# An S5 and pooling block on one core: one gate product moved into the readout, modulation rows and context norm issued earlier

## Chip, cores and metric

The kernel runs on one core of a Trainium2 chip (the other cores are idle). The metric is the device time of one execution in microseconds. In the views, PE is TensorE (PEld its weight loads), DVE is VectorE, ACT is ScalarE, POOL is GpSimd, SP is SyncE, which here only issues DMAs; the granted clock of TensorE is given as a share of 2.4 GHz.

## What is computed

One layer over 1024 latent tokens and 256 context tokens, 1024 channels wide, all in float32 (cut):

```python
h  = modulate(rms_norm(x, norm1_g), sh1, sc1)        # sh1, sc1, g1, ...: sections of silu(c) @ w_mod + b_mod
hc = modulate(rms_norm(ctx, norm1_g), csh1, csc1)
proj, proj_c = h @ w_in, hc @ w_in[:, :512]          # w_in 1024 x 3072
u_a, u_b, gate_a, gate_b = split(proj, [512, 1024, 2048])
st_f, st_b = s5_states(u_a, ...)                     # complex diagonal scan, seeded from the context
y = gelu((c_f . st_f + c_b . st_b).real + d * u_a)   # "readout"
y_a = (y * sigmoid(y @ w_glu + b_glu)) @ w_branch_a  # "GLU", then branch a
y_b = pool_mixer(u_b) @ w_branch_b                   # windowed means, 4 products with pool_w, branch b
x = x + g1 * ((sigmoid(gate_a) * y_a + sigmoid(gate_b) * y_b) @ w_out)
x = x + g2 * swiglu(modulate(rms_norm(x, norm2_g), sh2, sc2), w_ffn_in, w_ffn_out)
out = rms_norm(x, final_norm_g)
```

## The kernel before

Channels lie on partitions, tokens on the free axis, in two halves of 512. Every float32 product is made of three products of rounded parts: each operand is split into a high part (an ACT copy with rounding) and a low part (a DVE subtraction), and `mm3` issues high by high, high by low and low by high (L264, L266, L268; 128x512 each).

**Weights.** `Weights` goes through a list of jobs (one DMA each) and of units (one rounding each: ACT L97, DVE L98), laid down in `weight_order`. `take(ahead)` hands out the next rounded unit and rounds further ones until `ahead` units are ready behind it. When the last unit of a job is rounded, `load` issues the DMA of the next job (L79, on SP). There are two raw buffers, and five `wt` buffers for rounded weights.

**Order.** The program is scheduled by hand: each engine does its instructions in the order in which the code is written. Work that runs beside a product is written as Python generators ("side"): a product calls `next(side)` after each of its k steps. DMAs are issued on the SP and ACT queues, each in order. Each hardware DMA takes the next of eight completion semaphores, which the two queues share, so an issue also waits until the DMA eight issues before it has landed.

**Stages** (times of the span). *Startup* (0 to 85 us): `x` is loaded, normed and transposed; rows of the modulation (`mod_rows(kp)`, matmuls L543 from `wm` tiles, three buffers, loaded by `load_mod`, L494) and columns (`mod_cols`, L553, then DVE L558) give the modulated `h` (ACT L470 and L471, DVE L472), and products `mm(kt, q)` (L579) with slabs of `w_in` (L501, three buffers) follow tile by tile. *Input projection* (to about 210): pooling, context norm (`scale_ctx` puts its DVE operations in a queue that `drain(n)` empties by n) and the matrices of the scan (`mats`). *Scan* to 350, with gate products `gate("b", ...)` and `gate("a", 0, 4)`, each eight k steps of `mm3`, two sigmoids (ACT L1316) and two stores (L1317, ACT queue). *Readout*, 351 to 383: `f_phase(m)` for m of 0 to 3, 48 small matmuls each (L1339 from `U` and `M`, L1341 from `Fw` and the states `V`), gelu (ACT L1343) into one tile `y`, and eight stores of `y` (L1348, SP queue). `Fw`, `M` and `U` have two buffers each, so `f_loads(m + 2)` is issued when phase m has read its own. *Late gates*, 387 to 445: gates a4 to a7, each followed by one pooling product `pool_mm`; beside them `tiles` loads and splits sixteen halves of the pooled differences `d` and of `y` (loads L1360, ACT L1366, DVE L1367), and `sections` does steps of modulation sections 2 to 4 (load of 256 KB from `w_mod`, three ahead, into one of eight `ld` buffers, then DVE L1428 or L1430). *Branches*, 445 to 550: four GLU products (L1513 to L1516: sigmoid; DVE add of the two parts of y; DVE multiplication; split), then eight rounds of branch b and branch a products and the merge, with section steps beside them; `gather_sections` in round 3 needs 32 steps done. *Output projection and SwiGLU* to the end.

Of the kernel before, what the change touches and what calls it, by code (L numbers as in the profile page):

```python
# [235 lines left out]
class Kernel:  # L236
# [81 lines left out]
    def run(self):  # L318
# [36 lines left out]
        with self.pool("fpool", side="right") as fp:  # L355
            loads = [self.f_loads(fp, m) for m in range(2)]
            self.gate("a", 0, 4, side)
            for _ in side:
                pass
            for m in range(4):  # L360
                self.f_phase(fp, m, loads)
        par.close()
        vs.close()
        self.ap1 = es.enter_context(self.pool("acts1", side="right"))
# [10 lines left out]
    def weight_order(self):  # L375
        W = self.W8 = Weights(self)
        cols = lambda w, c, n: w[:, c:c + n].rearrange("(k p) m -> p k m", p=128)
        two = [(0, 0), (0, 128)]
        w_in = self.w_in[0]
        W.units += W.job([cols(w_in, 896, 128)], 8, 128, [(0, 0)])  # L380
        for c in list(range(0, 512, 256)) + list(range(2048, 3072, 256)) + list(range(1024, 2048, 256)):
            W.units += W.job([cols(w_in, c, 256)], 8, 256, two)
            if c == 1280:
                W.units += W.job([self.pool_w[0].rearrange("j c m -> c j m")], 4, 128, [(0, 0)])
        W.units += W.job([cols(self.w_glu[0], 0, 512)], 4, 512, [(0, i * 128) for i in range(4)])
        for c in range(0, D, 256):
            W.units += W.job([cols(w[0], c, 256) for w in (self.w_branch_b, self.w_branch_a)], 4, 256,
                             [(s, i) for i in (0, 128) for s in (0, 1)])
# [85 lines left out]
    def startup(self, hs):  # L474
# [166 lines left out]
        scale(7, nc.scalar)  # L641
        load_slab(3)
        mm(0, 0)
        mm(1, 0)
        for u in self.ub:
            u.append(self.psum())
# [4 lines left out]
        slab(2)  # L651
        self.drain(10)
        mm(0, 1)
        mod_rows(1)
        load_mod(2, 0)
        load_mod(2, 1)
        self.s5_load_b()
        self.s5_load_c()
        trans(2, 0)
# [93 lines left out]
    def input_proj(self):  # L753
# [26 lines left out]
        pooling = pool_steps()  # L780
        for kt, q in ((6, 1), (7, 0), (7, 1)):
            self.mm_ub(kt, q)
            next(mats)
            self.drain(5)
        begin(0, self.ub[0])
        begin(1, self.ub[1])

# [542 lines left out]
    def f_phase(self, fp, m, loads):  # L1330
        nc = self.nc
        Fw, M, U = loads[m]
        y = fp.tile([128, 8, 128], F32, name="y")
        for hf in range(2):
            p = self.psum()
            for i in range(4):
                g = hf * 4 + i
                o = p[:, i * 128:i * 128 + 128]
                nc.tensor.matmul(o, M[:, i, hf], U[:, g], start=True, stop=False, skip_group_check=True)  # L1339
                for d in range(2):  # L1340
                    nc.tensor.matmul(o, Fw[:, d, g], self.V[d][:, d:d + 8, m * 8 + g, 0:16],  # L1341
                                     start=False, stop=(d == 1), skip_group_check=True)
            nc.scalar.activation(y[:, hf * 4:hf * 4 + 4].rearrange("p j (b i) -> p j i b", b=16),  # L1343
                                 p.rearrange("p (j i b) -> p j i b", j=4, b=16), AF.Gelu_apprx_tanh)
        if m < 2:
            loads.append(self.f_loads(fp, m + 2))
        for t in range(8):
            nc.sync.dma_start(self.yT[m][:, t].rearrange("(g c) n -> c g n", c=16), y[t * 16:t * 16 + 16])  # L1348


    def at1(self, dt=F32R):
# [92 lines left out]
    def late_gates(self):  # L1444
# [5 lines left out]
        def tiles():  # L1450

            srcs = []
            for kind, j in todo:
                for q in range(2):
                    srcs.append((kind, j, q, self.dT[j][:, q * 512:q * 512 + 512] if kind == "d" else
                                 self.yT[j][:, q * 4:q * 4 + 4].rearrange("p t n -> p (t n)")))
            got = [self.ld(srcs[i][3]) for i in range(3)]
            for i, (kind, j, q, _) in enumerate(srcs):
                if i + 3 < len(srcs):
# [15 lines left out]
        tiles = tiles()  # L1475
        sections = self.mod_sections((2, 3, 4))

        def side(n, m):
            for i in range(8):
                if i % 2 == 0 and i // 2 < n:  # L1480
                    next(tiles, None)
                elif m > 3 or i > 5:
                    next(sections, None)
                yield

        ph, pl = self.W8.take()
        for _ in range(2):
            next(tiles)
        for m in range(4, 8):
            self.gate("a", m, m + 1, side(4, m))  # L1490
            pool_mm(m - 4)
        self.sections = sections
        self.ys = [ys[m] for m in range(4)]

    def branch(self, acts, left, side=None):
        wh, wl = self.W8.take(min(2, left))
        ps = [self.psum() for _ in range(2)]
        for k in range(4):
            self.mm3(ps, wh[:, k], wl[:, k], acts[k], k == 0, k == 3)
            if side and k % 2:  # L1500
                next(side, None)
        return ps

    def branches(self):
        nc = self.nc

        ya = []
        for m in range(4):
            ps = self.branch(self.ys, 2, self.sections)
            ts = []  # L1510
            for q in range(2):
                t, u = self.ld(), self.ld()
                nc.scalar.activation(t, ps[q], AF.Sigmoid, bias=self.cols[:, 84 + m:85 + m])  # L1513
                hi, lo = self.ys[m][q]
                nc.vector.tensor_tensor(u, hi.bitcast(F32), lo.bitcast(F32), op=OP.add)
                nc.vector.tensor_tensor(t, t, u, op=OP.mult)  # L1516
                ts.append(t)
            ya.append([self.split_a(t, self.at2) for t in ts])
        merged = []
# [583 lines left out]
```

## Time and profile before

| | |
|---|---|
| runs before | median 1316.56 us of 3 (1312.87 to 1317.75) |
| profiled execution | 1315.17 us; span 1313.4 us |
| granted clock of TensorE, mean | 0.988 |
| busy PE, PEld, DVE, ACT, POOL | 1246.1, 1005.1, 948.5, 531.4, 13.4 us |
| HBM read, written | 168.67 MB, 70.00 MB |

The span reaches from the first to the last instruction; the execution's own time has 1.8 us more. Busy time counts an engine's own instructions. "Idle before, releaser" is the idle time of an engine just ahead of an instruction, and what ended it. A window row gives busy time per engine in a stretch, the mean granted clock there and the share of the DMA engines.

### The profile page before, as it was taken

What the parts mean: (1) busy time and instruction counts of PE and PEld (TensorE: products, weight loads), DVE (VectorE), ACT (ScalarE), POOL (GpSimd) and SP (SyncE); (2) the same over time, 40 slices, a digit from 0 to 9 for tenths busy, and PEclk for the clock granted to TensorE, in tenths of its full rate; (3) what the DMA queues carried; (4) which work ended last, traced back from release to release, by engine and by line L of the source; (5) the groups of instructions that cost most, each with busy time, mean ns of one, the idle gap of its engine ahead of it and who ended that gap; (6) DMA issues with size and microseconds to landing.
All of it is one profiled execution on the core that took longest, in us unless ns stands there. A gap on an engine that the chain in (4) does not pass through costs nothing.

```text
span 1313.4 us, 16704 instructions
## 1 busy us (share of the span) xinstructions
PE 1246.1 (95%) x5811; PEld 1005.1 (77%) x5811; DVE 948.5 (72%) x1778; ACT 531.4 (40%) x951; POOL 13.4 (1%) x36
## 2 busy tenths in 40 slices
PE   6888989999969999999999999999999999999996
PEld 4567757878868788788887788888888888888884
DVE  7779983899606696855679977678778766578576
ACT  5564214742225521222574333333333345454443
POOL 4000000000000000000000000000000000000000
PEclk8999999999989999999999999999999999999998
DMA  8624569126477665653514733676666539776543
GB/s 286 182 97 162 180 184 339 65 81 216 145 183 251 208 211 189 209 175 111 199 35 141 235 107 108 147 233 206 227 209 203 175 126 321 272 227 194 189 144 129
DMA packets 196428, 239.79 MB, mean 183 GB/s; under 512 B 16928, under 2 KB 117880, under 8 KB 195832
## 3 DMA queue, kind: packets, MB, share of 16 engines
q1 hardware_dynamic: 188200, 222.92, 52.8%
q10 hardware_dynamic: 8144, 15.80, 3.2%
q8 instruction: 46, 0.75, 0.2%
q14 instruction: 38, 0.31, 0.1%
HBM read 168.67 MB, written 70.00 MB: 182 GB/s over the span
## 4 chain that ended last, share of the span: by engine, by line
PE 59%; DVE 19%; DMA 9%; ACT 7%; issue 4%; SPq 1%; ACTq 0%; DVEq 0%
PE ps L1724 10%; PE ps L1722 10%; PE ps L1723 9%; PE ps L1953 5%; PE ps L1954 5%; PE ps L1952 5%; PE ps L268 2%; PE ps L264 2%; PE ps L266 2%; PE ps L1568 2%; PE ps L1566 2%; PE ps L1567 2%; DMA wm<-in_w_mod_dram 1%; DVE wt L98 1%; DMA Md<-kb 1%
## 5 line engine op out<-in xcount | busy, mean ns | idle before, releaser
L1722 PE MATMUL ps<-a,wt 128*128 128x512 f32 x436 | 172.7, 396 | 2.4 <-ACT ld L1836 2.4
L1724 PE MATMUL ps<-a,wt 128*128 128x512 f32 x436 | 171.5, 393 | 0.3 <-DVE wt L124 0.3
L1723 PE MATMUL ps<-a,wt 128*128 128x512 f32 x436 | 170.6, 391 | 0.0
L124 DVE TENSOR_TENSOR a<-a,a 128x512 fp32r<-128x512 f32 x162 | 103.3, 685 | 30.9 <-ACT a L225 30.2
L1953 PE MATMUL ps<-a,a 128*128 128x512 f32 x308 | 122.0, 396 | 1.1 <-DVE a L124 1.1
L1952 PE MATMUL ps<-a,a 128*128 128x512 f32 x308 | 121.8, 396 | 0.0
L1954 PE MATMUL ps<-a,a 128*128 128x512 f32 x308 | 121.8, 396 | 0.0
L264 PE MATMUL ps<-h,wt 128*128 128x512 f32 x336 | 109.0, 405 | 5.1 <-ACT wt L97 4.7
L268 PE MATMUL ps<-h,wt 128*128 128x512 f32 x336 | 105.4, 395 | 2.0 <-DVE wt L98 1.9
L266 PE MATMUL ps<-h,wt 128*128 128x512 f32 x336 | 105.0, 394 | 0.0
L225 ACT ACTIVATE a<-a 128x512 fp32r<-128x512 f32 x154 | 87.1, 624 | 42.9 <-DVE a L124 13.2
L1722 PEld LDWEIGHTS ps<-a,wt 128*128 128x128 f32 x436 | 81.8, 188 | 21.1 <-ACT ld L1836 3.3
L1724 PEld LDWEIGHTS ps<-a,wt 128*128 128x128 f32 x436 | 81.9, 188 | 20.4 <-DVE wt L124 1.2
L1723 PEld LDWEIGHTS ps<-a,wt 128*128 128x128 f32 x436 | 82.0, 188 | 18.4
L1366 ACT ACTIVATE a<-ld 128x512 fp32r<-128x512 f32 x64 | 39.3, 629 | 128.4 <-DVE ld L1543 64.9
L264 PEld LDWEIGHTS ps<-h,wt 128*128 128x128 f32 x336 | 60.3, 190 | 19.9 <-ACT wt L97 5.7
L268 PEld LDWEIGHTS ps<-h,wt 128*128 128x128 f32 x336 | 60.8, 189 | 16.6 <-DVE wt L98 4.6
L266 PEld LDWEIGHTS ps<-h,wt 128*128 128x128 f32 x336 | 61.7, 190 | 12.5
L98 DVE TENSOR_TENSOR wt<-raw,wt 128x1024 fp32r<-128x1024 f32 (+1 forms) x42 | 39.8, 951 | 43.5 <-ACT wt L97 43.4
L1953 PEld LDWEIGHTS ps<-a,a 128*128 128x128 f32 x308 | 57.9, 188 | 15.8 <-DVE a L124 1.9
L1952 PEld LDWEIGHTS ps<-a,a 128*128 128x128 f32 x308 | 57.9, 188 | 14.0
L1954 PEld LDWEIGHTS ps<-a,a 128*128 128x128 f32 x308 | 57.9, 188 | 13.9
(336 smaller groups left out, 2456.0 us busy)
## 6 DMA issues: line engine op xcount, KB each, us to landing
raw<-in_w_ffn_in_dram SPq DMA_DIRECT2D x44, 512.0 KB
ld<-in_w_mod_dram SPq DMA_DIRECT2D x64, 256.0 KB
a<-in_w_ffn_out_dram SPq DMA_DIRECT2D x55, 256.0 KB
raw<-in_w_in_dram SPq DMA_DIRECT2D x10, 1024.0 KB
wm<-in_w_mod_dram SPq DMA_DIRECT2D x16, 512.0 KB
ld<-in_w_ffn_out_dram SPq DMA_DIRECT2D x22, 256.0 KB
x<-in_x_dram SPq DMA_DIRECT2D x8, 512.0 KB
ETd<-out ACTq DMA_DIRECT2D x16, 256.0 KB
```

What stands on the lines that cost most here:

```text
L98: nc.vector.tensor_tensor(lo, src, hi.bitcast(F32), op=OP.subtract)
L124: self.K.nc.vector.tensor_tensor(lo, self.src, hi.bitcast(F32), op=OP.subtract)
L225: K.nc.scalar.activation(hi, t, AF.Copy)
L264: nc.tensor.matmul(o, wh, ah, start=first, stop=False)
L266: nc.tensor.matmul(o, wh, al, start=False, stop=False)
L268: nc.tensor.matmul(o, wl, ah, start=False, stop=last)
L1722: nc.tensor.matmul(p, wh, ah, start=first and k == 0, stop=False, skip_group_check=on)
L1723: nc.tensor.matmul(p, wh, al, start=False, stop=False, skip_group_check=on)
L1724: nc.tensor.matmul(p, wl, ah, start=False, stop=last and k == 3, skip_group_check=on)
L1952: nc.tensor.matmul(p, ah[:, s], wh, start=first and i == 0, stop=False, skip_group_check=on)
L1953: nc.tensor.matmul(p, ah[:, s], wl, start=False, stop=False, skip_group_check=on)
L1954: nc.tensor.matmul(p, al[:, s], wh, start=False, stop=i == NB - 1, skip_group_check=on)
```

## The change

It does six things. (1) In `startup`, `mod_rows(1)` and the loads for `mod_rows(2)` are written between `mm(0, 0)` and `mm(1, 0)` instead of behind `mm(0, 1)`. (2) In `weight_order`, the four pooling weights are a unit between those of gates a4 and a5 instead of ahead of both. (3) In `input_proj`, eight queued operations of the context norm are drained ahead of each matrix step, instead of five behind it. (4) In `run`, gate a4 is issued inside the readout, behind phase 1, with two units ready behind the one it takes; `f_phase` writes `y` to one of three parts of `work` (a buffer of the scan that is free by then) and issues its eight stores on SP and ACT in turn. (5) `late_gates` has gates a5 to a7, beside each five tile steps (before: four) and three section steps, a7 with three units ready behind it. (6) In `branches`, the multiplier `u` of the GLU is loaded from `yT`, instead of added up from the two parts by DVE, and one section step stands behind each multiplication.

```diff
@@ run
             for m in range(4):
                 self.f_phase(fp, m, loads)
+                if m == 1:
+                    self.gate("a", 4, 5, None, 2)
@@ weight_order
-            if c == 1280:
-                W.units += W.job([self.pool_w[0].rearrange("j c m -> c j m")], 4, 128, [(0, 0)])
+            if c == 1536:
+                W.units[-1:-1] = W.job([self.pool_w[0].rearrange("j c m -> c j m")], 4, 128, [(0, 0)])
@@ startup
         mm(0, 0)
+        mod_rows(1)
+        load_mod(2, 0)
+        load_mod(2, 1)
         mm(1, 0)
...
         mm(0, 1)
-        mod_rows(1)
-        load_mod(2, 0)
-        load_mod(2, 1)
@@ input_proj
             self.mm_ub(kt, q)
+            self.drain(8)
             next(mats)
-            self.drain(5)
@@ f_phase
-        y = fp.tile([128, 8, 128], F32, name="y")
+        y = self.work.rearrange("p a q -> p (a q)")[:, m % 3 * 1024:m % 3 * 1024 + 1024].rearrange(
+            "p (g n) -> p g n", g=8)
...
-            nc.sync.dma_start(self.yT[m][:, t].rearrange("(g c) n -> c g n", c=16), y[t * 16:t * 16 + 16])
+            (nc.scalar if t % 2 else nc.sync).dma_start(
+                self.yT[m][:, t].rearrange("(g c) n -> c g n", c=16), y[t * 16:t * 16 + 16])
+
+    def y_half(self, m, q):
+
+        return self.yT[m][:, q * 4:q * 4 + 4].rearrange("p t n -> p (t n)")
@@ late_gates
-        def side(n, m):
+        def side():
             for i in range(8):
-                if i % 2 == 0 and i // 2 < n:
+                if i % 2 == 0 or i == 7:
                     next(tiles, None)
-                elif m > 3 or i > 5:
+                else:
                     next(sections, None)
                 yield
...
-        for m in range(4, 8):
-            self.gate("a", m, m + 1, side(4, m))
-            pool_mm(m - 4)
+        for m in range(5, 8):
+            self.gate("a", m, m + 1, side(), 3 if m == 7 else 1)
+            pool_mm(m - 5)
+        for _ in tiles:
+            pass
+        pool_mm(3)
@@ branches
+        us = [self.ld(self.y_half(0, q)) for q in range(2)]
         for m in range(4):
...
-                t, u = self.ld(), self.ld()
+                t, u = self.ld(), us[q]
                 nc.scalar.activation(t, ps[q], AF.Sigmoid, bias=self.cols[:, 84 + m:85 + m])
-                hi, lo = self.ys[m][q]
-                nc.vector.tensor_tensor(u, hi.bitcast(F32), lo.bitcast(F32), op=OP.add)
                 nc.vector.tensor_tensor(t, t, u, op=OP.mult)
+                if m < 3:
+                    us[q] = self.ld(self.y_half(m + 1, q))
+                next(self.sections, None)
```

How this moves the instructions, at three places. The rows are each engine's instructions in order: line, operation, out<-in, elements; a number behind a name tells one tile from another. Lines of the changed kernel are up to twelve higher: its gelu is L1346, its sigmoid L1318, the stores of `y` L1351.

SP in the startup, before (`wm`: modulation weights; `slab`: a slab of `w_in`; `raw`: scan parameters):

```order
L494 DMA wm<-in_w_mod_dram 128x4x256 x2
L501 DMA slab<-in_w_in_dram 128x384 x3
L494 DMA wm<-in_w_mod_dram 128x4x256 x4
L901 DMA raw<-in_s_b_re_dram 64x1024
L901 DMA raw<-in_s_b_im_dram 64x1024
```

Here the four loads for `mod_rows(2)` stand behind three slab loads. Of the change:

```order
L496 DMA wm<-in_w_mod_dram 128x4x256 x2
L503 DMA slab<-in_w_in_dram 128x384 x2
L496 DMA wm<-in_w_mod_dram 128x4x256 x4
L503 DMA slab<-in_w_in_dram 128x384
L903 DMA raw<-in_s_b_re_dram 64x1024
```

They now stand ahead of the third slab load.

ACT in the readout and just behind it, before (`y`: gelu results; `wt<-raw`: rounding of weights, 1024 wide for a gate; `a<-ld`: the split of a tile):

```order
L1343 ACT_TABLE_LOAD
L1343 ACTIVATE y<-ps 128x4x8x16 x8
L97 ACTIVATE wt<-raw 128x1024
L1366 ACTIVATE a_3471<-ld 128x512
L1366 ACTIVATE a_3477<-ld 128x512
L97 ACTIVATE wt<-raw 128x1024
```

ACT does the eight gelus in a row, with no DMA issue between them, and rounds a4's weights behind them. Of the change, from the stores of phase 1:

```order
L1351 DMA yT_89<-work 16x8x128 x4
L97 ACTIVATE wt<-raw 128x512
L97 ACTIVATE wt<-raw 128x1024
L1318 ACT_TABLE_LOAD
L1318 ACTIVATE tmp<-ps 128x512
L1319 DMA siga_246<-tmp 128x512
L1318 ACTIVATE tmp<-ps 128x512
L1319 DMA siga_246<-tmp 128x512
L1346 ACT_TABLE_LOAD
L1346 ACTIVATE work<-ps 128x4x8x16 x2
L1351 DMA yT_90<-work 16x8x128 x4
L1346 ACTIVATE work<-ps 128x4x8x16 x2
```

Half of the stores of `y`, two roundings and a4's two sigmoids, with two more table loads, now stand between the gelus.

DVE beside one GLU product, before (`ld<-a,a`: the two parts of y added up; `ld<-ld`: the multiplication; L1430: a section step):

```order
L1515 TENSOR_TENSOR ld<-a_3620,a_3621 128x512
L1516 TENSOR_TENSOR ld<-ld 128x512
L1515 TENSOR_TENSOR ld<-a_3641,a_3642 128x512
L1516 TENSOR_TENSOR ld<-ld 128x512
L1367 TENSOR_TENSOR a_3996<-ld,a_3995 128x512
L1367 TENSOR_TENSOR a_4000<-ld,a_3999 128x512
L98 TENSOR_TENSOR wt<-raw,wt 128x512
L1430 SCALAR_TENSOR_TENSOR a_3966<-ld,cols,a_3966 128x512 x2
```

Of the change:

```order
L1526 TENSOR_TENSOR ld<-ld 128x512
L1438 SCALAR_TENSOR_TENSOR a_3854<-ld,cols,a_3854 128x512
L1526 TENSOR_TENSOR ld<-ld 128x512
L1438 SCALAR_TENSOR_TENSOR a_3854<-ld,cols,a_3854 128x512
L1375 TENSOR_TENSOR a_3980<-ld,a_3979 128x512
L1375 TENSOR_TENSOR a_3984<-ld,a_3983 128x512
L98 TENSOR_TENSOR wt<-raw,wt 128x512
L1438 SCALAR_TENSOR_TENSOR a_3854<-ld,cols,a_3854 128x512 x2
```

Two section steps took the places of the two additions.

## Rows read from the trace of the kernel before

**Rows 1.** The page: busy time by engine, and the chain of waits by engine.

```profile
PE 1246.1 (95%) x5811; PEld 1005.1 (77%) x5811; DVE 948.5 (72%) x1778; ACT 531.4 (40%) x951; POOL 13.4 (1%) x36
...
PE 59%; DVE 19%; DMA 9%; ACT 7%; issue 4%; SPq 1%; ACTq 0%; DVEq 0%
```

**Rows 2.** Timeline of PE in the readout: start us, us, instruction [idle before <-releaser].

```profile
365.10 0.46 PE L1339 MATMUL ps<-U,M 128*128 128x128 f32 x2 [2.84 <-DMA U<-uT]
...
374.39 0.77 PE L1339 MATMUL ps<-U,M 128*128 128x128 f32 x2 [3.70 <-DMA U<-uT]
...
387.13 1.01 PE L264 MATMUL ps<-h,wt 128*128 128x512 f32 x2 [4.19 <-ACT wt L97]
```

**Rows 3.** Windows: us, busy of each engine (x instructions), PE clock, DMA share, GB/s.

```profile
351.38:356.73 5.35, 5.35 (x49) 5.35 (x48) 0.00 (x0) 3.55 (x4) 0.00 (x0) 1.00 0.75 269
374.39:382.94 8.55, 8.54 (x48) 8.35 (x48) 0.00 (x0) 2.02 (x2) 0.00 (x0) 0.64 0.44 68
387.13:399.75 12.62, 12.62 (x48) 10.22 (x49) 4.32 (x5) 3.74 (x6) 0.00 (x0) 0.86 0.72 181
401.14:412.07 10.93, 10.93 (x49) 9.01 (x48) 5.06 (x8) 5.57 (x8) 0.00 (x0) 1.00 0.96 336
445.61:473.10 27.49, 27.49 (x120) 22.58 (x121) 26.07 (x42) 12.76 (x22) 0.00 (x0) 1.00 0.42 137
```

**Rows 4.** Timeline of PE in the startup.

```profile
45.02 2.34 PE L579 MATMUL ps<-h,wt 128*128 128x512 f32 x9
...
51.74 1.07 PE L543 MATMUL ps<-wm,ccols 128*32 128x512 f32 x8 [2.95 <-DMA wm<-in_w_mod_dram]
52.74 3.91 PE L579 MATMUL ps<-h,wt 128*128 128x512 f32 x9
```

**Rows 5.** Chain of waits in the startup: start us, us, what.

```profile
38.56 1.90 PE ps L543 x16
...
40.70 10.99 DMA wm<-in_w_mod_dram
```

**Rows 6.** Timeline of DVE in the startup.

```profile
57.47 0.22 DVE L558 TENSOR_SCALAR mods<-ps,cols 128x2 f32<-128x2 f32 x1 [2.31 <-PE ps L553]
```

**Rows 7.** Windows, same columns: the startup, and the input projection.

```profile
30.00:40.00 10.00, 8.63 (x44) 5.43 (x42) 6.73 (x32) 5.56 (x9) 0.00 (x0) 0.88 0.09 25
...
85.00:160.00 75.00, 65.82 (x369) 52.09 (x368) 73.79 (x120) 29.75 (x58) 0.00 (x0) 0.98 0.44 154
```

**Rows 8.** Timeline of ACT, readout and late gates.

```profile
353.39 1.28 ACT L1343 ACT_TABLE_LOAD   x1 [0.39 <-ACT tmp L1316]
354.68 1.10 ACT L1343 ACTIVATE y<-ps 128x512 f32<-128x512 f32 x1
...
393.35 1.23 ACT L1366 ACTIVATE a<-ld 128x512 fp32r<-128x512 f32 x2 [6.28 <-DMA ld<-dT]
...
404.72 0.60 ACT L1316 ACTIVATE tmp<-ps 128x512 f32<-128x512 f32 x1
...
406.75 0.69 ACT L1471 ACTIVATE tmp<-ps,cols 128x512 f32<-128x512 f32 x1 [0.41 <-ACT tmp L1316]
...
410.91 0.69 ACT L1471 ACTIVATE tmp<-ps,cols 128x512 f32<-128x512 f32 x1 [2.80 <-DMA siga<-tmp]
```

**Rows 9.** Timeline of SP, readout and late gates (us: until the last of the group was issued).

```profile
369.33 20.55 SPq L1348 DMA_DIRECT2D yT<-y  x24
```

**Rows 10.** Timeline of DVE in the GLU products.

```profile
445.07 0.69 DVE L1367 TENSOR_TENSOR a<-tmp,a 128x512 fp32r<-128x512 f32 x1 [1.64 <-ACT a L1366]
...
469.60 1.47 DVE L1367 TENSOR_TENSOR a<-ld,a 128x512 fp32r<-128x512 f32 x2
```

**Rows 11.** Groups by line: out<-in xcount | busy us, mean ns | idle before.

```profile
L1367 DVE TENSOR_TENSOR a<-ld,a 128x512 fp32r<-128x512 f32 x64 | 43.4, 689 | 29.3 <-ACT a L1366 28.1
L1430 DVE SCALAR_TENSOR_TENSOR a<-ld,cols,a 128x512 f32<-128x512 f32 x56 | 41.8, 747 | 2.4 <-DMA ld<-in_w_mod_dram 1.7
```

**Rows 12.** Waits by line: us in total, times, longest us.

```profile
DVE a L1428 <- DMA ld<-in_w_mod_dram: 8.3, 2, 6.1
```

More of the change, by code (lines that the diff above doesn't have):

```diff
@@ L1455, in tiles @@
                     srcs.append((kind, j, q, self.dT[j][:, q * 512:q * 512 + 512] if kind == "d" else
-                                 self.yT[j][:, q * 4:q * 4 + 4].rearrange("p t n -> p (t n)")))
+                                 self.y_half(j, q)))
             got = [self.ld(srcs[i][3]) for i in range(3)]
@@ L1499, in branch @@
             self.mm3(ps, wh[:, k], wl[:, k], acts[k], k == 0, k == 3)
-            if side and k % 2:
+            for _ in range(k % 2 if side else 0):
                 next(side, None)
```

## Prediction

> **What bounds the kernel now.** I read the page first. PE is busy 1246.1 of 1313.4 us and has 59% of the chain, DVE 19% [rows 1]. So over most of the span only fewer or quicker PE instructions would help, and the change takes none away: it can only win where PE idles or runs at the lower clock. I therefore looked in PE's timeline for its gaps beside the edited code. There are three in and behind the readout: 2.84 and 3.70 us for `U`, 4.19 us for a weight that ACT rounds [rows 2]. A readout phase takes 5.35 us at a granted clock of 1.00, but the one that stands behind the gap of 3.70 took 8.55 at 0.64, and gate a4 behind the gap of 4.19 took 12.62 at 0.86, where the next gate with its pooling weights ready took 10.93 [rows 3]. There is one gap in the startup, 2.95 us, with a product behind it of 3.91 us instead of 2.34 [rows 4]. Whether another engine would keep up with a PE without these gaps is read from ACT's and DVE's timelines [rows 8, 10].
>
> **Startup (part 1).** The chain there goes from the rows of `mod_rows(1)` through SP to a load of 10.99 us, and PE waits for it [rows 5]: the load is issued when a `wm` buffer is read, at 40.5. Behind `mm(0, 0)` the same matmuls can start at about 33.4, some 5 us earlier. They wait for nothing new, since the DMA engines are 9% busy from 30 to 40, with the earlier rows' loads landed [rows 7]. The load then starts some 5 us earlier, more than the wait of 2.95, and SP, which moves it ahead of a slab that must wait for its buffer, is otherwise idle. The slab comes later in the queue by four issues, about 2 us, and is the sixth of eight, needed only by `mm(5, 0)`, three tiles on. Upper end: 2.95 + (3.91 - 2.34) = 4.5 us. Lower end: DVE, which makes the `h` that PE consumes, has only its own idle of 2.31 us to lose [rows 6]. I take 3.5, nearer the upper end, because PE, not DVE, stands in the chain there.
>
> **Context norm (part 3).** Zero. From 85 to 160 us DVE is busy 73.79 of 75.00 us [rows 7] and the same operations are only reordered on it; PE's idle there is DVE's backlog. It would be worth a microsecond or two only if a PE wait moved off an instruction that comes late on DVE; I keep that for the range.
>
> **Readout (parts 2, 4), PE's side.** With gate a4 behind phase 1, PE does 10.93 us of work from about 362 to 373. In it the third `U` lands (365.10 in the trace of before) and the fourth nearly does (374.39). The weight of a4 was rounded long before, that of a5 is rounded during a4, so the third gap goes as well. Gone at most: 2.84 + 3.70 + 4.19 = 10.7 us of waits, 8.55 - 5.35 = 3.2 and 12.62 - 10.93 = 1.7 us of lower clock. With the wait at the end of the late gates for ACT's last items (DVE's idle there is 1.64 [rows 10], PE's about the same), which a PE that ran in step with earlier loads would not have, **17.2 us**. This is the upper end of the part.
>
> **Readout and late gates, ACT's and DVE's side.** Here the sum is smaller, since ACT and DVE have their own chain from the first split of a `d` tile at 393.35 to the last pooling split, which ends at 445.07 + 0.69 = 445.8 [rows 8, 10]: 52.4 us, of which ACT spends much waiting for loads and for stores that free a `tmp`. PE can't shorten it. What does: the first `d` load is issued behind the stores of `y`, 24 of which hold SP for 20.55 us, since each needs phase 3's gelu or a free semaphore [rows 9]. Phase 3 ends little earlier than before (its `U` lands at 374.4 still), but 12 of the 24 issues are on ACT's queue now; I give it 2.3 us, to 391. Gate a4's sigmoids and stores leave the stretch, 404.72 to 406.75 = 2.0, and with them one wait of a later ACT instruction on such a store, 2.80 [rows 8]. Roundings balance (one of a gate out, two small GLU units in). So the last pooling split ends near 445.8 - 2.3 - 2.0 - 2.8 = 438.7.
>
> Then the GLU stage, DVE bound: 26.07 us busy of 27.49 [rows 3]. Before, it ran from 445.8 to 469.60 + 1.47 = 471.1, 25.3 us [rows 10]. Now DVE has 16 section steps (14 at 0.747, two first ones near 0.48: 11.4), 8 multiplications and 8 splits of the shape of 0.689 (11.0) and three roundings (2.1): 24.5 us [rows 11]. **Part 6** thus takes away 8 additions of 0.69 (5.5) and brings 8 steps (6.0): no gain here, but eight steps fewer later, where PE is the bound and DVE idle, so nothing there. Its 8 loads of 256 KB hide beside the products. To this I add 2 us for section loads that come late: four steps per product now follow a prefetch of three, and SP has the branch weights in front of them. Ends: 0, and 6.1, the longest wait of such a step [rows 12]. The last GLU split so ends at 438.7 + 24.5 + 2 = 465.2 instead of 471.1, a gain of **5.9 to 6.1 us**; PE, up to 17 us ahead, waits for it in the first branch a product. From there to the end the relation of the engines is as before, and PE carries the gain on.
>
> **More table loads.** The gate between the gelus costs two more switches of ACT's table, 1.28 us each; the gelu behind the load starts at 354.68, 0.01 us after its end [rows 8]. Both lie where ACT waits anyway, so I count nothing. The Trainium skill, ScalarE: Activation LUTs, section What ACT_TABLE_LOAD costs, adds a drain of about 1.38 us to each load (2.66 in all), a rule against such a placing. This trace shows no drain behind the load; by the page the two would cost an estimated 5.3 us of ACT instead of 2.6, which would take up to 2.7 us off the gain if they were not hidden.
>
> **The sum.** 3.5 + 6.0 = 9.5 us, off the profiled execution: 1315.17 - 9.5 = 1305.7. The median of the runs is 1.4 us above that execution, so I say **1306**. A measurement of this kernel can tell about 0.5% (6.6 us) from no change.
>
> **Rivals.**
> 1. *ACT and DVE keep up* and PE's whole gain comes: 3.5 + 17.2 = 20.7, 1295 to 1296. For it: most of ACT's stretch is waits for loads and stores, which may all start earlier. Against: the split of the last pooled tile must follow sixteen tile splits and seven other items in ACT's fixed order, and DVE is 95% busy in the GLU stage. 0.17.
> 2. *Little is left.* The `d` loads come no earlier (they need the last stores' semaphores), or the new wait of PE in branch a brings the lower clock that followed earlier gaps of 3.70 and 4.19 (1.7 to 3.2 us more), or the startup gives only 2.3. The late region then gives 0 to 4, in all 2 to 6: 1310 to 1314, within 0.5%. 0.21.
> 3. *Slower: section loads as the new wait.* In the GLU stage DVE does four section steps per product with three loads ahead. SP issues in order, and has the branch weight loads and the `u` loads in front of them. If each of the four products had one wait of 6.1 us [rows 12], DVE would lose 24 us. Against that stand the startup's 3.5 and the late region's 445.8 - 438.7 + 25.3 - 24.5 = 7.9: 1316.6 - 3.5 - 7.9 + 24 = 1329. It decides from about 11 us of such waits on (no change), and from 18 us the kernel is slower by 0.5%. Against: the first steps of a section waited only twice in the trace of before [rows 12]. 0.07.
> 4. *The change does not do what it says*: that is so of the context norm in any case, and counted. That a4 doesn't cover the loads of `U` would need them to land 9 us later than before; their issue hangs on phases 0 and 1, which stay. Under 0.02, inside rival 2.
>
> **How the numbers follow.** The forecast has 0.55, with a range of its own from 1301 (no late section load, startup 4.5, SP earlier) to 1310. Faster by over 0.5% (below 1310): nearly all of 0.55 and 0.17, 0.71. Within: 0.21 and a little of the third rival, 0.22. Slower: 0.07. The range leaves out the third rival and the outer half of the first: **1297 to 1314**.
>
> **What the next profile would show.** Startup: no wait of about 3 us before the matmuls of `mod_rows(2)`, and no product at 3.9 us behind it. Readout: four phases of 5.4 us each and gate a4 of 10.9 between the second and third, all at a clock of 1.00, no wait of PE from 351 to 384. Late gates: PE ahead of ACT by more than 10 us, first `d` split near 391 less the startup's 3.5, last pooling split near 438.7 less 3.5. GLU: DVE without idle but for waits on section loads, PE waiting 5 us or more for a split of `ya` in the first branch a product. I'd be wrong if PE idles nowhere behind the readout (rival 1), if ACT's first split of `d` is not earlier (rival 2), or if DVE waits on `ld` from `w_mod` over 3 us per product (rival 3).

## The result, and the profile after

The changed kernel takes **1307.44 us** (median of 5 runs, 1303.18 to 1307.91), the kernel before 1316.83 (median of 5) beside it: ratio 0.9916, 95% interval 0.9895 to 0.9936, so 8 to 14 us less. The forecast was 1306, with 1297 to 1314. The executions of one kernel differ by several us, and the one profiled here, 1307.91 us, was the slowest of its five.

The page of the changed kernel (profiled execution 1307.91 us, span 1306.1), parts 1 and 4, beside [rows 1]:

```profile
PE 1245.0 (95%) x5811; PEld 1002.5 (77%) x5811; DVE 943.4 (72%) x1770; ACT 535.2 (41%) x953; POOL 12.7 (1%) x36
...
PE 55%; DVE 21%; DMA 10%; ACT 6%; issue 4%; SPq 2%; ACTq 0%; DVEq 0%
```

PE does the same work. It holds 55% of the chain instead of 59%; DVE and DMAs hold what it lost. So over a longer part of the span the chain now goes through DVE and the loads, not through PE.

Startup, timeline of PE, beside [rows 4] (the lines of the code are two higher):

```profile
46.98 1.92 PE L545 MATMUL ps<-wm,ccols 128*32 128x512 f32 x16
48.84 2.34 PE L581 MATMUL ps<-h,wt 128*128 128x512 f32 x9
```

All sixteen matmuls of `mod_rows(2)` run in a row, and the product behind them takes 2.34 us, not 3.91. Readout, windows of the phases 0 and 1, gate a4, and the phases 2 and 3, beside [rows 2, 3]:

```profile
346.82:357.46 10.64, 10.64 (x98) 10.63 (x96) 0.00 (x0) 4.66 (x5) 0.00 (x0) 1.00 0.51 173
357.46:368.46 11.00, 11.00 (x52) 9.10 (x51) 0.00 (x0) 2.60 (x3) 0.00 (x0) 1.00 0.88 271
368.46:379.09 10.63, 10.63 (x97) 10.63 (x96) 1.92 (x2) 6.97 (x8) 0.00 (x0) 1.00 0.96 301
```

No idle time, clock 1.00 throughout: the three gaps are gone. PE is done with readout and a4 at 379.09, where before it was done at 399.75, 20.7 us earlier. Of these, 4.6 came from ahead of the readout (346.82 against 351.38). At the end 7.3 us of span are left. Where the rest went is seen in PE's timeline from there to the output projection:

```profile
391.64 0.51 PE L264 MATMUL ps<-a,wt 128*128 128x512 f32 x1 [1.39 <-ACT a L1374]
393.00 0.50 PE L264 MATMUL ps<-a,wt 128*128 128x512 f32 x1 [0.86 <-ACT a L1374]
...
424.06 0.98 PE L264 MATMUL ps<-a,wt 128*128 128x512 f32 x2 [1.84 <-ACT wt L97]
...
452.81 1.22 PE L268 MATMUL ps<-a,wt 128*128 128x512 f32 x2 [3.82 <-DVE wt L98]
...
519.49 0.74 PE L268 MATMUL ps<-a,wt 128*128 128x512 f32 x2 [1.65 <-DVE wt L98]
```

and in the windows that begin with the first of these waits, the third and the fourth:

```profile
391.64:397.43 5.79, 4.93 (x13) 3.44 (x13) 3.85 (x6) 3.99 (x6) 0.00 (x0) 0.71 0.98 355
424.06:428.04 3.98, 3.98 (x10) 3.15 (x11) 3.98 (x8) 3.55 (x7) 0.00 (x0) 0.57 0.06 13
452.81:458.76 5.95, 5.95 (x15) 4.65 (x15) 5.77 (x10) 2.98 (x6) 0.00 (x0) 0.52 0.77 266
```

The waits sum to 9.6 us. At the full clock a matmul of this shape takes 11.00 / 48 = 0.229 us (window of a4, which has 8 k steps of 6 matmuls), so 13, 10 and 15 of them should take 3.0, 2.3 and 3.4 us; they took 4.9, 4.0 and 6.0, together about 6.2 more. Of 9.6 + 6.2 = 15.8 the kernel before had 1.61 + 1.09 in the same stretch (its timeline, not shown above):

```profile
445.61 0.74 PE L264 MATMUL ps<-a,wt 128*128 128x512 f32 x2 [1.61 <-ACT wt L97]
...
543.94 0.44 PE L1402 MATMUL ps<-ident,a 128*128 128x128 f32 x2 [1.09 <-DVE a L1392]
```

That leaves 13.1 of the 20.7 us given back, about what separates them from the 7.4 us by which the output projection now starts earlier (547.8 against 555.2). The windows of the whole stretch up to it, before and of the change, give the same without counting waits one by one:

```profile
399.75:555.20 155.45, 152.19 (x704) 122.86 (x703) 115.63 (x188) 54.17 (x90) 0.00 (x0) 1.00 0.65 214
```

```profile
379.09:547.80 168.71, 158.93 (x705) 126.88 (x704) 112.16 (x182) 58.52 (x95) 0.00 (x0) 0.96 0.67 221
```

For the same matmuls PE is busy 6.7 us longer, at a clock of 0.96 instead of 1.00, and idle 6.5 us longer (9.8 instead of 3.3).

What made PE wait, from the chain of waits (start us, us, what):

```profile
371.96 10.59 DMA raw<-in_w_glu_dram
...
444.01 6.37 DMA ld<-in_w_mod_dram
...
501.91 10.18 DMA gd<-cols
```

Each is a link of its own, and the timelines of ACT (first two lines) and DVE show them:

```profile
383.49 2.11 ACT L1346 ACTIVATE work<-ps 128x512 f32<-128x512 f32 x2 [7.11 <-DMA yT<-work]
...
390.96 0.63 ACT L1374 ACTIVATE a<-ld 128x512 fp32r<-128x512 f32 x1 [5.35 <-DMA ld<-dT]
```

```profile
436.29 0.69 DVE L1375 TENSOR_TENSOR a<-tmp,a 128x512 fp32r<-128x512 f32 x1 [0.55 <-ACT a L1374]
...
450.47 0.49 DVE L1436 TENSOR_SCALAR a<-ld,cols 128x512 f32<-128x512 f32 x1 [3.92 <-DMA ld<-in_w_mod_dram]
...
462.41 1.29 DVE L1375 TENSOR_TENSOR a<-ld,a 128x512 fp32r<-128x512 f32 x2
...
517.47 1.37 DVE L1545 TENSOR_TENSOR ld<-ps,ld 128x512 f32<-128x512 f32 x2 [9.60 <-DMA ld<-sigb]
```

PE ended phase 3 at 379.09, but its gelu began at 383.49, since ACT stood 7.11 us in its own queue. Two of its stores of `y` could only be issued at 382.57, when the load of the GLU weights had landed (371.96 + 10.59 = 382.55). So the first `d` split came at 390.96. In the GLU stage DVE stood 3.92 us at a section step; the rounding for the first branch b product is queued behind it, and PE waited for that. The third link is a store of one modulation section (`gd`), which takes 10.18 us to land (the kernel before has the same store, and waits 9.67 us for it on SP); the row that is read back from it stands on SP ahead of the next gate loads, and DVE waits 9.60 us for these.

### The profile page after: what moved, and what is told of

It reads as the page before. It is cut to its first block, busy times and chain, and to the rows that moved or that the text cites. A ratio compares the mean times of both kernels' runs of the same rounds, so it can differ in the third digit from the quotient of the medians.

```text
span 1306.1 us, 16703 instructions
## 1 busy us (share of the span) xinstructions
PE 1245.0 (95%) x5811; PEld 1002.5 (77%) x5811; DVE 943.4 (72%) x1770; ACT 535.2 (41%) x953; POOL 12.7 (1%) x36
## 4 chain that ended last, share of the span: by engine, by line
PE 55%; DVE 21%; DMA 10%; ACT 6%; issue 4%; SPq 2%; ACTq 0%; DVEq 0%
PE ps L1735 10%; PE ps L1737 10%; PE ps L1736 9%; PE ps L1966 5%; PE ps L1967 5%; PE ps L1965 5%; DMA ld<-in_w_mod_dram 2%; PE ps L1579 2%; PE ps L1581 2%; PE ps L1580 2%; DVE wt L98 2%; DMA U<-uT 1%; DVE V L1262 1%; PE ps L264 1%; PE ps L268 1%
## 5 line engine op out<-in xcount | busy, mean ns | idle before, releaser
L1375 DVE TENSOR_TENSOR a<-ld,a 128x512 fp32r<-128x512 f32 x64 | 43.1, 690 | 45.2 <-ACT a L1374 44.4
L1966 PEld LDWEIGHTS ps<-a,a 128*128 128x128 f32 x308 | 57.9, 188 | 15.8 <-DVE a L124 1.9
```

The lines of the kernel that those rows point to most:

```text
L1375: self.nc.vector.tensor_tensor(lo, src, hi.bitcast(F32), op=OP.subtract)
L1966: nc.tensor.matmul(p, ah[:, s], wl, start=False, stop=False, skip_group_check=on)
```

## The experiments

Each ran in five rounds (e2: once) beside runs of the kernel before, e5 to e8 on another chip than the other experiments; the ratio is always to the runs beside it. No run has part 2, 4, 5 or 6 alone: e9 moves the gate of part 4, e3 and e8 undo half of part 6. Stage lengths come from the first and last start of a line's matmuls in the profiled execution. "Readout to projection" is from the first readout matmul to the first matmul of the output projection.

| run | readout starts | readout to projection | median us | ratio to before (95%) |
|---|---|---|---|---|
| before | 351.4 | 203.8 | 1316.83 | |
| change | 346.8 | 201.0 | 1307.44 | 0.9916 (0.9895 to 0.9936) |
| e1 startup part alone | 346.3 | 205.6 | 1314.61 | 0.9956 (0.9941 to 0.9971) |
| e2 context norm alone | 353.8 | 205.5 | 1320.13 | one run; before 1320.48 |
| e3 additions put back | 348.9 | 202.4 | 1313.29 | 0.9952 (0.9935 to 0.9969) |
| e4 twelve steps | 345.0 | 208.0 | 1315.03 | 0.9960 (0.9944 to 0.9975) |
| e5 change again | 346.6 | 196.1 | 1306.09 | 0.9925 (0.9904 to 0.9946) |
| e6 both weight loads held | 346.2 | 200.8 | 1309.67 | 0.9943 (0.9921 to 0.9964) |
| e7 steps in the late gates | 347.0 | 201.7 | 1310.70 | 0.9952 (0.9935 to 0.9968) |
| e8 additions, no u loads | 347.1 | 202.7 | 1312.00 | 0.9959 (0.9943 to 0.9975) |
| e9 gate a4 behind phase 3 | 349.4 | 203.3 | 1310.81 | 0.9932 (0.9911 to 0.9952) |
| e10 branch weights held | 347.5 | 201.5 | 1309.68 | 0.9923 (0.9908 to 0.9938) |
| e11 GLU weights held | 346.8 | 197.6 | 1307.14 | 0.9911 (0.9896 to 0.9926) |
| e12 both holds | 345.9 | 198.4 | 1307.09 | 0.9908 (0.9892 to 0.9923) |

The two executions of the changed kernel differ by 4.9 us in the second column, so one execution's stage length alone decides nothing below that; the first was the slowest of its five, that of e5 the fastest of its six.

**e1: the startup part alone.** On the kernel before:

```diff
         mm(0, 0)
+        mod_rows(1)
+        load_mod(2, 0)
+        load_mod(2, 1)
         mm(1, 0)
...
         mm(0, 1)
-        mod_rows(1)
-        load_mod(2, 0)
-        load_mod(2, 1)
```

> The kernel before with part 1 of the change alone (modulation rows 1 and the loads for rows 2 behind the first product). My account: the readout of the changed kernel begins 4.56 us earlier (346.82 against 351.38), and it is this part that does it: span of the profiled run 4 to 5 us shorter than 1313.4, so about 1309, time ratio near 0.9965. Rival: part of the 4.56 us comes from the context norm, and PE only gets the 2.3 us that DVE had idle: span near 1311. Second rival: later waits in the readout swallow it (the loads of U wait for a fixed thing): no change.

The readout began at 346.3, 5.1 us earlier, so the startup part alone explains the 4.6 of the changed kernel. The time's ratio is 0.9956, so 4 to 8 us less. The span of the profiled execution, 1313.0, isn't near the 1309 that was expected: it lost 1.8 us up to the projection and 2.9 behind it. One execution differs by as much from another, so the ratio decides here. In the readout the gaps are as before, which keeps the two terms apart:

```profile
360.07 0.46 PE L1339 MATMUL ps<-U,M 128*128 128x128 f32 x2 [2.89 <-DMA U<-uT]
...
369.69 0.77 PE L1339 MATMUL ps<-U,M 128*128 128x128 f32 x2 [4.02 <-DMA yT<-y]
...
382.42 1.07 PE L264 MATMUL ps<-h,wt 128*128 128x512 f32 x2 [4.23 <-ACT wt L97]
```

**e2: the context norm alone.** On the kernel before:

```diff
+            self.drain(8)
             next(mats)
-            self.drain(5)
```

> The kernel before with part 3 alone (eight operations of the context norm drained ahead of each matrix step). My account: nothing, span within 0.5 us of 1313.4, since DVE is busy 73.79 of 75.00 us from 85 to 160; the first PE wait there (2.89 us at 95.44) changes its place and not the sum. Rival: it takes that wait away, span 2 to 3 us shorter.

The time did not move (1320.13 beside a median of 1320.48), so no gain is seen; one execution can exclude neither a gain nor a loss of a few us. Its trace also shows that the startup's wait is not the same each time: here the load for `mod_rows(2)` was in time with the old order.

```profile
49.41 1.92 PE L543 MATMUL ps<-wm,ccols 128*32 128x512 f32 x16
51.26 2.35 PE L579 MATMUL ps<-h,wt 128*128 128x512 f32 x9
```

Even so its readout starts 2.4 us later than before: the matrices of the scan are 1.5 us ahead of it at 162.06 and 1.7 behind at 184.89, with a PE wait of 3.15 us for DVE between (169.31). Whether part 3 or chance did that, one execution doesn't show; the changed kernel, which has part 3 too, starts its readout when e1 does.

**e3 and e8: what the swapped additions are worth.** On the changed kernel, e3 puts the additions back and keeps the loads of `u`; e8 has the additions and no loads:

```diff
                 t, u = self.ld(), us[q]
+                hi, lo = self.ys[m][q]
                 nc.scalar.activation(t, ps[q], AF.Sigmoid, bias=self.cols[:, 84 + m:85 + m])
+                nc.vector.tensor_tensor(u, hi.bitcast(F32), lo.bitcast(F32), op=OP.add)
                 nc.vector.tensor_tensor(t, t, u, op=OP.mult)
```

> The changed kernel with the eight DVE additions of part 6 put back (u is still loaded, then overwritten by the sum of the two parts; same result), all section steps kept. If DVE bounds the GLU stage of the changed kernel, as I hold: 8 x 0.69 = 5.5 us more on DVE there, PE's wait in the first branch b product grows from 3.82 to 8 or 9 us, span 4 to 6 us longer than 1306.1. Rival: the stage is bound by the section loads (the one wait of 3.92 us on them), so the additions fill DVE's wait: 0 to 2 us longer.

> The changed kernel with u added up by DVE as before and without its eight loads (2 MB), all section steps kept. If the GLU stage is bound by loads (the DMA engines were 86% busy from 447 to 460): the late section load of 3.92 us goes, DVE has 5.5 us more: about no change, and 1 to 2 us shorter than with additions and loads. If DVE bounds it: 4 us longer than the changed kernel.

e8 ran beside the changed kernel (e5) and took 5.9 us more by the medians; e3's ratio is 0.0027 above e5's, about 3.6 us. Leaving the loads out did not help (0.9959 against 0.9952). So DVE's instructions bound the GLU stage, and 8 x 0.69 = 5.5 us on it cost 3.6 to 5.9 us of time; that the loads are the bound fell. With the additions back the ratio is about that of the startup part alone (0.9956). The PE waits, instead of one of 3.82, were many small ones for ACT and DVE, of which in e8:

```profile
442.99 0.73 PE L264 MATMUL ps<-a,wt 128*128 128x512 f32 x2 [1.59 <-ACT wt L97]
...
450.37 0.74 PE L264 MATMUL ps<-a,wt 128*128 128x512 f32 x2 [1.21 <-ACT wt L97]
453.54 1.22 PE L268 MATMUL ps<-a,wt 128*128 128x512 f32 x2 [1.97 <-DVE wt L98]
...
466.86 0.50 PE L264 MATMUL ps<-a,wt 128*128 128x512 f32 x1 [1.59 <-ACT a L1374]
```

**e4: three steps per GLU product instead of four.**

```diff
-                next(self.sections, None)
+                if q:
+                    next(self.sections, None)
...
         for _ in tiles:
             pass
+        next(sections)
```

> The changed kernel with a section step behind the second multiplication only (three per GLU product instead of four), and one step moved ahead of the last pooling product. My account: the late section load (3.92 us of DVE's wait) is needed one step later or more and DVE has 3 steps (2.2 us) less to do, so DVE ends the stage 4 to 6 us earlier, PE's wait of 3.82 in the first branch b product and the lower clock behind it go: span 4 to 6 us shorter than 1306.1, near 1301. Rival: the wait only moves to a later round, where the second gather needs all steps: no change, within 1 us.

The expected gain didn't come, and the kernel was slower than the change (0.9960), more than the rival said. The wait in the first branch b product went, but the step that the second gather needs was now the last one done, and PE stood for it:

```profile
533.87 0.66 PE L1397 MATMUL ps<-a,ones 128*32 128x128 f32 x8 [10.16 <-DVE a L1438]
```

So the steps beside the GLU are not spare work: they pay for a later gather.

**e7: steps in the late gates.** Two steps at each section slot of the late gates, none behind the GLU's multiplications:

```diff
                 else:
                     next(sections, None)
+                    next(sections, None)
...
-                next(self.sections, None)
                 ts.append(t)
```

> The changed kernel with six section steps beside each late gate instead of three (DVE is busy 5 of 10 us there) and none behind the GLU multiplications (two per GLU product as before). My account: the GLU stage has 8 steps less (6.0 us of DVE, 2 MB of loads), so PE's wait of 3.82 in the first branch b product and the lower clock go; the late gates' tile loads come a little later: span 3 to 5 us shorter. Rival: the loads only compete with the tile loads instead, ACT's waits in the late gates grow by as much: no change.

Nothing was won, as the rival said, and by the medians 4.6 us were lost (1310.70 beside 1306.09), which it did not say. The wait in the first branch b product is gone, and in its place PE waits in the late gates, where ACT rounds later:

```profile
411.52 1.22 PE L264 MATMUL ps<-h,wt 128*128 128x512 f32 x2 [3.15 <-ACT wt L97]
...
430.17 0.73 PE L264 MATMUL ps<-a,wt 128*128 128x512 f32 x2 [2.06 <-ACT wt L97]
```

**e5: the change again.**

> The changed kernel as it is, beside the next three on one chip, as their base. My account: time ratio to before 0.991 to 0.993 again; from the start of the readout to the output projection 201 us (before 203.8); PE's waits of 1 to 2 us at the first pooling product and the first GLU product and near 4 us in the first branch b product recur. If the wait of 3.82 us was a disturbance of one execution, it is missing here.

Ratio 0.9925, as expected; from the readout to the projection it took 196.1 us, not the 201 expected. The late waits recur, smaller: 1.39 and 0.48 us for the `d` splits, none of note at the first GLU product, and

```profile
449.58 0.73 PE L268 MATMUL ps<-a,wt 128*128 128x512 f32 x2 [2.25 <-DVE wt L98]
```

with the matmuls behind it at full speed (clock 1.00 from 449.58 to 455.00). So the wait is no disturbance, but its size varies, and the clock fell behind it in one execution and not in the other: this execution keeps 7.7 us of the late region (203.8 - 196.1), the first one 2.8.

**e6 and e11: the weights loaded inside the readout, held.** e6 holds both loads of 1 MB until the first four `d` loads are issued, e11 only that of the GLU weights (e6 lacks the condition on `glu`, the number of that load). Of e11, cut:

```diff
+        self.hold, self.held = False, 0
...
+    def release(self, hold=False):
+        self.hold = hold
+        n, self.held = self.held, 0
+        for _ in range(n):
+            self.load()
+
     def load(self):
         if self.loaded == len(self.jobs):
+            return
+        if self.hold and self.loaded >= self.glu:
+            self.held += 1
+            return
...
                 if m == 1:
+                    self.W8.hold = True
                     self.gate("a", 4, 5, None, 2)
...
+        W.glu = len(W.jobs)
...
-        for _ in range(2):
-            next(tiles)
+        next(tiles)
+        self.W8.release()
+        next(tiles)
```

> The changed kernel, with the two weight loads of 1 MB that are issued at 371 (inside the readout) held until the first four loads of d tiles are issued. My account: they keep the semaphores that phase 2's and 3's stores need (10.59 us for the GLU weights in the chain), ACT stands in its queue for 6.96 us and the last gelu starts at 383.5; held, it starts near 380, the first split of d at 387 to 388 instead of 390.96, PE's wait at the first pooling product (1.39 + 0.86 and a lower clock) shrinks by 2 to 4 us, span 2 to 4 us shorter. Rival 1: the d tiles wait for memory traffic anyway, and the held loads now hold up the rounding of the gate's weights: no change, or 1 to 3 us longer. Rival 2: all that is won there is lost at the section loads behind: no change.

> The changed kernel with only the GLU weights' load (1 MB, 371.96, 10.59 us in the chain) held until the first four d loads are issued; the gate weights' load stays. In the run that held both, the last gelu no longer waited, but PE then waited 2.18 and 1.49 us for the gates' rounding. My account: the gelu starts at 380 to 381, the gates' rounding is in time, PE's waits in the late gates fall from 1.9 to 2.3 us in sum to under 1: 0 to 3 us shorter than the changed kernel. Rival: the stores wait for the other weights' load as long: no change.

e6: the last gelu began at 377.87 instead of 383.49 and the first `d` split at 385.38, but PE waits for gate weights that come late, as its first rival said, and then 4.25 us in the first branch b product, behind a section load, as its second said. The time is not shorter:

```profile
393.17 0.73 PE L274 MATMUL ps<-h,wt 128*128 128x512 f32 x2 [2.18 <-ACT wt L107]
...
407.63 0.73 PE L274 MATMUL ps<-h,wt 128*128 128x512 f32 x2 [1.49 <-ACT wt L107]
```

e11: the gelu began at 379.71 and the first `d` split at 387.54 instead of 390.96, which shows that the GLU weights' load was what ACT's queue waited for. PE's wait at the pooling product is gone, but one stands at the next gate (one of 2.52 us in the first branch b product stays), and the time (0.9911) can't be told from the changed kernel's.

```profile
406.89 0.81 PE L274 MATMUL ps<-h,wt 128*128 128x512 f32 x2 [2.96 <-ACT wt L107]
```

**e9: gate a4 behind phase 3.**

```diff
-                if m == 1:
+                if m == 3:
                     self.gate("a", 4, 5, None, 2)
```

> The changed kernel with gate a4 behind phase 3 instead of phase 1, all else kept. It tells what the place inside the readout is worth by itself. My account: PE's waits for U return (2.84 + 3.70 us, with 3.2 us of lower clock), PE's lead of 14.3 us at the first GLU product shrinks to about 4, but since ACT, DVE and loads set the end of the GLU stage, only part of the 10 us reaches the end: 3 to 7 us longer than the changed kernel (ratio to before 0.995 to 0.998). Rival 1: the place is what the whole late gain hangs on: 10 us longer, ratio 1.000. Rival 2: the chain of ACT and DVE is the bound all along and PE's lead is worth nothing: within 1 us of the changed kernel, 0.992.

```profile
363.84 0.53 PE L1342 MATMUL ps<-U,M 128*128 128x128 f32 x2 [3.51 <-DMA U<-uT]
...
374.45 0.77 PE L1342 MATMUL ps<-U,M 128*128 128x128 f32 x2 [3.39 <-DMA yT<-work]
...
458.23 1.22 PE L268 MATMUL ps<-a,wt 128*128 128x512 f32 x2 [4.24 <-DVE wt L98]
```

The gaps for `U` return, and the readout-to-projection stretch is 203.3, 2 to 7 us longer than the two executions of the change. The time's ratio, 0.9932, lies within the intervals of the change (0.9916, 0.9925). By the ratios the place is worth 1 to 2 us, with intervals that overlap; by one stage length 2 to 7. The 3 to 7 us of my account (ratio 0.995 to 0.998) are not seen in the time, which is nearer the second rival's 0.992. A loss of 10 us (ratio 1.000) is excluded: PE's gaps, back in full, cost the time little. Whether the place by itself is worth anything stays open. The first wait behind the readout is then the same section load at 458.

**e10 and e12: the branch weights held.** e10 holds the second load of branch weights until the GLU products are issued, e12 is e10 and e11 together. The hold of e10 has no condition; of its edit, cut:

```diff
         us = [self.ld(self.y_half(0, q)) for q in range(2)]
+        self.W8.hold = True
...
+        self.W8.release()
         merged = []
```

> The changed kernel, with the second load of branch weights (2 x 512 KB, issued in the GLU stage at 443 ahead of section loads) held until the GLU products are issued. If DVE's late section load (3.92 us in one execution, 2.3 in another) is a load queued behind these weights: the wait falls below 1 us, PE's wait in the first branch b product (3.82, 2.25) goes, from the start of the readout to the output projection 194 to 197 us (201.0 and 196.1 before), 1 to 4 us shorter in time. Rival: the wait comes from the three-deep prefetch and stays, or the held weights are late for round 2: no change or longer.

> The changed kernel with both of these holds. If the two waits are separate links of the same chain, the gains add: 2 to 6 us shorter than the changed kernel, ratio to before 0.988 to 0.991. If the chain is then set by something behind it (loads of the rounds, the second gather), no more than the better one alone.

e10 did what it should where it should: no wait in the first branch b product. But from the readout to the projection it took 201.5 us, not the 194 to 197 expected. PE waited 1.73 and 2.08 us at the first pooling product, and DVE and PE met the third link:

```profile
516.73 1.37 DVE L1557 TENSOR_TENSOR ld<-ps,ld 128x512 f32<-128x512 f32 x2 [10.79 <-DMA ld<-sigb]
```

```profile
499.98 0.38 SPq L1430 DMA_DIRECT2D gd<-cols  x1
511.29 0.33 SPq L1459 DMA_DIRECT2D g1row<-gd  x1
511.70 0.86 SPq L1378 DMA_DIRECT2D ld<-sigb  x2
```

```profile
518.75 1.22 PE L278 MATMUL ps<-a,wt 128*128 128x512 f32 x2 [4.33 <-DVE wt L108]
```

SP issues nothing from 500.4 to 511.3, since the read of `gd` must wait for the store to land; the gate loads behind it come late. PE's 4.33 us stand where the kernel before has 0.31 and the changed kernel 1.65. e12 has the lowest ratio (0.9908), but its interval overlaps the change's, and it is no better than e11 alone (0.9911): no sum of gains is seen. In its trace, too, DVE waits 10.43 us at 513.07 and PE 3.99 at 515.10, behind the same store. That this wait takes what was won ahead of it fits both traces; no run without the store tests it.

## Why the prediction was right

The time fell, and by about the sum, 3.5 + 6.0 = 9.5 us: 9.4 by the medians, 11 by the ratio, 10 in e5. The main choice was right, that ACT's and DVE's chain and not PE's gaps would set the late gain: from 351 to 400 PE won 16.1 us (15.6 of the 17.2 said at most lay there), and 2.8 of them were left at the projection in one execution, 7.7 in another. e9, which gives PE its gaps back, costs 1 to 2 us by the ratios, with intervals that overlap. That the sum was met so closely is luck, though: two of its terms were off, in opposite directions. By the ratios, e1 is worth 5.8 us and the rest of the change 4 to 5, where 3.5 and 6.0 were said. Nor is 1306 quite the sum: taken off the median, as the text there wants it, 9.5 us leave 1316.56 - 9.5 = 1307.1.

The late chain can be taken apart at three instructions: the first `d` split, the last pooling split and the last GLU split. For the change they are shown above (390.96, 436.29 and 462.41, the last two with the durations beside them); in e5 they are

```profile
390.75 0.63 ACT L1374 ACTIVATE a<-ld 128x512 fp32r<-128x512 f32 x1 [5.61 <-DMA ld<-dT]
```

```profile
434.63 0.69 DVE L1375 TENSOR_TENSOR a<-tmp,a 128x512 fp32r<-128x512 f32 x1 [0.55 <-ACT a L1374]
...
459.52 1.29 DVE L1375 TENSOR_TENSOR a<-ld,a 128x512 fp32r<-128x512 f32 x2
```

| us | before | said | change | e5 |
|---|---|---|---|---|
| readout's start to first `d` split | 42.0 | 39.7 | 44.1 | 44.2 |
| to the end of the last pooling split | 52.4 | 47.6 | 46.0 | 44.6 |
| to the end of the last GLU split | 25.3 | 26.5 | 26.7 | 25.5 |

- **Startup**, 3.5 said, 4.6 and 5.1 found. Upper end, not the value taken: the lower end rested on DVE's idle of 2.31 [rows 6], which was no bound. e2 shows that the wait was not in every execution.
- **Context norm**, 0 said, none seen (e2, one run; and the changed kernel starts its readout no earlier than e1).
- **Readout on PE**: as said, window by window. The wait of 1.6 us at the end of the late gates, also counted as gone, is there in one execution (1.84 at 424.06) and nearly gone in e5 (0.25).
- **First `d` split**: said to come 2.3 us earlier in the readout, it came 2.2 later, the wrong way; this step failed. I put half of the stores on ACT's queue as a help to SP, and did not cost that ACT itself stands there (7.11 us), behind a 1 MB load which gate a4's roundings issue. e11 moved it to 387.54.
- **Late gates**: 4.8 us were said to leave the stretch with gate a4's sigmoids and a wait for its stores; 6.4 and 7.8 left it, which made up for a third and for two thirds of what the term before lost. Why more left was not tested.
- **GLU stage**: DVE bound, as said (e3, e8), and 26.7 and 25.5 us long, where 26.5 was said. The late section loads, put at 2 us, were 3.92 and 2.34. Only PE's wait was in another place: the first branch b product, whose rounding stands on DVE behind that step. I had it in branch a. With it came, in one of two executions, the lower clock that rival 2 named.
- **More table loads**: two loads of 1.28 us, counted as nothing; ACT stood 7.11 us for a load soon after the second, so it had that time to spare. In the changed kernel the gelu of phase 2 starts 0.02 us after the load's end, and ahead of the load ACT is idle for 0.41 us. The drain of about 1.38 us that the Trainium skill, ScalarE: Activation LUTs, section What ACT_TABLE_LOAD costs, adds to each load does not show in these rows:

```profile
373.06 1.28 ACT L1346 ACT_TABLE_LOAD   x1 [0.41 <-ACT tmp L1318]
374.36 2.02 ACT L1346 ACTIVATE work<-ps 128x512 f32<-128x512 f32 x2
```

- **What I did not name**: the store and reload of the modulation row at 500 to 512. It is in the kernel before too, but PE only reaches it as a wait once it is early.

Rival 3's late section loads did occur, but in the GLU stage once per execution, at 3.92 and 2.34 us, and not four times at 6.1, so DVE lost 2 to 4 us and not 24.

## What to carry to other kernels

Work moved into a gap of PE gains what the next engine's chain leaves of it: price PE's lead at each later place where it meets another engine, not at the gap. When DMA issues are put on a computing engine's queue, count the time in which that engine stands in line for a free semaphore, and look what large load was issued shortly before. Background steps that a later gather needs can't simply be thinned out (e4), and moving them earlier can cost as much elsewhere (e7).

## What the runs showed of the hardware

The granted clock did not follow the length of the wait alone. Behind 1.84 us (424.06) the window shows 0.57, mostly the lower of the two levels (1.2 GHz, a clock of 0.50), though PE had been busy at 1.00 without a gap from 397.43 to 422.22. Behind 2.25 us in e5 and 2.84 in the kernel before (365.10 to 370.00) the clock stayed at 1.00, and behind 3.70, 4.19 [rows 2, 3] and 3.82 it fell. At the same place of the readout, a wait of 2.89 us kept 1.00 in e1 (360.07 to 365.00) and one of 2.88 gave 0.63 in e2 (367.51 to 372.00). What else decides is open. In the changed kernel the lower clock added 1.7 to 2.5 us each time, nearly as much as the waits.

And a 4 KB store whose elements lie apart (`gd`) took 10.18 us to land, as long as a load of 1 MB (10.59). Before the change and in e5 it took 9.67 and 9.74; in e10 SP's read of it was issued 11.3 us after the store. For most of that time no traffic shows: the DMA engines' share is 0.00 from 504 to 512 in the changed kernel. What takes the time is open.
